# Adding the experts' rows in DRAM, spreading transposes and narrowing the stick-breaking attention in a two-model kernel

## The chip, the cores and the metric

The kernel runs on one core of a Trainium2 chip. The metric is the device time of one execution in microseconds (us). TensorE is called PE, VectorE DVE, ScalarE ACT, GpSimd POOL and SyncE SP; POOL and SP also issue DMAs, each from a queue of its own.

## The reference, cut to what matters

256 tokens of 1024 features go through a first block of two attention layers and then through a second block of two layers. In the second block the first layer has stick-breaking attention and a dense SwiGLU, the second has a blockwise attention and a mixture of eight experts, two per token. The change touches the stick-breaking attention and the mixture of experts:

```python
def stick_breaking_attention(q, k, v):            # per query block, all heads
    z = einsum('bhqd,bhkd->bhqk', qc, k) * scale
    past = k_pos[None, :] < q_pos[:, None]        # a query sees only earlier keys
    log_one_minus = where(past, log_sigmoid(-z), 0.0)
    after = cumsum(log_one_minus, reverse=True) - log_one_minus
    w = where(past, exp(log_sigmoid(z) + after), 0.0)
    return einsum('bhqk,bhkd->bhqd', w, v)

def moe_swiglu(t, w_router, w1, w3, w2):
    top_val, top_idx = top_k(t @ w_router, 2)
    gates = softmax(top_val) spread over the 8 experts
    y = sum over e of ((silu(t @ w1[e]) * (t @ w3[e])) @ w2[e]) * gates[:, e]
h = h + y;  out = rmsnorm(h, final_norm)
```

With 256 tokens and keys in two tiles of 128, the queries 0 to 127 see no key of the second tile: that quarter of the 256 x 256 table is always masked.

## The kernel before

All products are made in float32 precision from two rounded parts of each operand: a high part (a cast by ACT, tile names ending in `h` or index 0) and a remainder (`sub_lo` on DVE, `gsub_lo` on POOL, a subtraction of two SBUF operands), with three matmuls for each product (`mm3`). Every weight tile is loaded by SP, cast by ACT (line 85) and subtracted by DVE or POOL (line 86), and then used by PE. Every engine takes its instructions in program order, so the order of the code sets the order of the work on each queue.

The stick-breaking stage (lines 1447 to 1535) works through 16 heads, the units, in a software pipeline: `pipeline` runs the stages in a fixed order for each iteration i, each stage for the unit i minus its lag. A unit's table is [128 keys, 512]: columns 0 to 255 are the 256 queries for key tile 0, columns 256 to 511 the same queries for key tile 1. `scores` puts a mask into PSUM by a matmul (`identr`, `smask`, 512 columns) and adds the score products of two heads; `soft` makes the softplus by three ACT steps; `softplus` (DVE) adds and casts (`u`, `uh`); `softplus_lo` makes the remainder `ul` on POOL; `sums` adds the running sums by two matmuls of 512 columns (`ntri`) and two of 256 (`nones`); `weights` is an exponential on ACT; `split` makes `whh` and `wll` on DVE; `pv` multiplies by the values in six matmuls of 256 columns into the single PSUM buffer `o`; `out` copies `o` out by ACT and DVE (`og`). As `fill`, PE does the rest of the query and key projections (24 matmuls of 256 columns in each of the first iterations, which POOL ends with the remainders of `qT` and `kT`), then the first part of the output projection.

The dense layer that follows also writes zeros to a DRAM buffer `ysum` of 640 rows (lines 1578 to 1581, POOL). The mixture of experts begins with routing (lines 1793 to 2059): `posm` is each token's place in its expert's list, `G` a one-hot table of the first two experts, and 32 matmuls gather those experts' tokens (`pieces`). Beside that, `x_natural` turns the residual `xT` into rows of tokens by PE transposes, and ACT copies them into `hnat`.

Then 57 steps n run, one for each expert e and seventh f of its hidden width: `first(n)` (48 matmuls of 512 columns), `second(n-1)` (24 matmuls), and `turn(n)` (4 transposes of `hf`, line 1980). Each step uses six 1 MB weight tiles out of 13 staging tiles and, later, `xT` as a fourteenth (`Stream.staging`, `wm.ahead`). Small jobs wait in the list `later`; `first` takes one from it after each of its 8 chunks, `second` three after each of its 4. Jobs on that list: `rows_table` and `rows_of` (which find each slot's token row and its factor), `choices` (the gates by rank, `granks`), and `fetched`, whose four pieces transpose the rows that POOL fetched for the next two experts, with an ACT copy and a DVE subtraction each. The results of experts 0 to 5 are copied by ACT (`y`) and written by POOL's indirect DMA into `ysum`, a token's better expert into rows 0 to 255, its other one into rows 256 to 511 (line 2005). In the last two steps both halves are loaded back (line 2085), and four DVE instructions multiply them by `granks` and add them to `hnat` (line 2089). Experts 6 and 7 are added to `hnat` by PE and DVE directly (`scatter`).

Of the kernel before, what the change touches and what calls it, by code (L numbers as in the profile page):

```python
# [7 lines left out]
F = mybir.dt.float32  # L8
# [24 lines left out]
class Stream:  # L33
# [67 lines left out]
def tile_net(  # L101
# [1349 lines left out]
    stk = pa.tile([128, 768], R, name="stk", bufs=1)  # L1451
    vcopy(stk, stf)
    identr = pa.tile([128, 128], R, name="identr", bufs=1)
    vcopy(identr, ident)
    ntri, nones, smask = stk[:, 0:128], stk[:, 128:256], stk[:, 256:768]

    class UnitS:
        def __init__(self, j, h):
            self.j, self.h = j, h

        def scores(self):
# [3 lines left out]
            for u in us:  # L1465
                u.S = ps2p.tile([128, 512], F, tag="s2", name="s2")
                mm(u.S, identr, smask, True, False)
            for k in range(2):
                both_heads([u.S[:, k * T:(k + 1) * T] for u in us], [a[:, self.j, k * 128:(k + 1) * 128] for a in kT],
                           [a[:, self.j, :] for a in qT], False, k == 1)  # L1470

        def soft(self):
            self.u = u = pa.tile([128, 512], F, tag="u", name="u", bufs=3)
# [4 lines left out]
        def softplus(self):  # L1478
            u = self.u
            self.uh = pa.tile([128, 512], R, tag="uh", name="uh")  # L1480
            self.ul = pa.tile([128, 512], R, tag="ul", name="ul")
# [3 lines left out]
        def softplus_lo(self):  # L1485
            gsub_lo(self.ul, self.u, self.uh)

        def sums(self):
            o = self.S
            for n, a in enumerate((self.uh, self.ul)):  # L1490
                nc.tensor.matmul(o, ntri, a, start=False, stop=False, skip_group_check=True)
                nc.tensor.matmul(o[:, 0:T], nones, a[:, T:2 * T], start=False, stop=n == 1, skip_group_check=True)

        def weights(self):
            self.w = pa.tile([128, 512], F, tag="w", name="w", bufs=3)
            act(self.w, self.S, ACTF.Exp)

        def split(self):
            self.wh = pa.tile([128, 512], R, tag="whh", name="whh")
            self.wl = pa.tile([128, 512], R, tag="wll", name="wll")  # L1500
# [30 lines left out]
    for n in range(0, 16, 2):  # L1531
        units[n].other = units[n + 1]
    pipeline(units,
             (("fill", 0), ("pv", 6), ("sums", 3), ("weights", 4), ("scores", 0), ("soft", 1), ("softplus", 2), ("softplus_lo", 2), ("split", 5), ("out", 6)), fill)
# [28 lines left out]
    ysum = scr.tile([2 * T + 128, D], F, name="ysum")  # L1563
# [47 lines left out]
    pe = mp.enter_context(pool("moef0"))  # L1611
    wm.tiles = [None] * NS + [xT.rearrange("p k n -> p (k n)")]
# [136 lines left out]
    vals = pm.tile([128, 2, 8, 3], F, name="vals")  # L1749
    tcol = pm.tile([128, 4], F, name="tcol")  # L1750
    granks = pm.tile([128, 2, 2], F, name="granks")
# [90 lines left out]
    x_natural(0)  # L1842
# [15 lines left out]
    def rows_table():  # L1858
# [7 lines left out]
        ts(w, tcol[:, 0:1], 2.0 * T, ALU.add)  # L1866
        for t in range(2):
            ts(vals[:, t, :, 0], rank[:, t], 0.0, ALU.mult, tcol[:, t:t + 1], ALU.add)
            ts(vals[:, t, :, 2], rank[:, t], 0.0, ALU.mult, nrm[:, t:t + 1], ALU.add)
            stt(vals[:, t, :, 1], rank[:, t], 1.0 * T, posm[:, t], ALU.mult, ALU.subtract)  # L1870
            ts(vals[:, t, :, 1], vals[:, t, :, 1], tcol[:, t:t + 1], ALU.add, -2.0 * T, ALU.add)

    def choices():
        for c_ in range(2):
            stt(ex, rank, float(c_), gate, ALU.is_equal, ALU.mult)
            nc.vector.reduce_sum(out=granks[:, c_, :], in_=ex, axis=AX.X)
# [3 lines left out]
    def rows_of(e, g):  # L1880

        ps = bank("tp")
# [359 lines left out]
```

## Time and profile before

| | |
|---|---|
| Runs of the kernel before, median (3 runs) | 2032.65 us (2031.85 to 2034.75) |
| Profiled execution, its own time | 2035.86 us |
| Span of that execution in the trace | 2034.0 us |
| PE busy | 1943.6 us, 96% |
| DVE busy | 1592.9 us, 78% |
| ACT busy | 1310.9 us, 64% |
| POOL busy | 310.8 us, 15% |
| DMA traffic | 505.91 MB, 249 GB/s on the mean |

The rows count time from the first instruction of the span. The dense and expert layers fill most of it: the stick-breaking stage lies at about 606 to 697 us, routing at 1030 to 1050 us, the expert steps from 1050 us to the end. A row of the timeline gives the start, the duration, the engine, the line, the operation with its output and inputs, and in brackets how long the engine sat idle before it and for whose result. Matmuls overlap each other, so PE's pace is read from the distance between starts and not from a duration.

### The profile page before, as it was taken

To read this page: it belongs to the slowest core of one execution; us is meant where nothing else is said; L and a number is where in the kernel's file an instruction comes from. 1 tells how busy PE (TensorE), PEld (TensorE's weight loads), DVE (VectorE), ACT (ScalarE), POOL (GpSimd) and SP (SyncE) were. 2 spreads that over 40 slices of the span, in tenths; PEclk is the share of its full clock that TensorE was granted. 3 is DMA by queue.
4 is the path that set the end of the run, shared out by engine and by line. 5 is a ranking of instruction groups with operands and counts; after the bars stand their busy time and mean duration, and the time that the engine had idled before them with its cause. 6 is when DMAs were issued, how large, how long until landed. Compare 5 with 4: busy or idle time off the path is not lost. (4 is left out here: it accounts for less than half of the span.)

```text
span 2034.0 us, 29605 instructions
## 1 busy us (share of the span) xinstructions
PE 1943.6 (96%) x10970; PEld 1647.7 (81%) x10970; DVE 1592.9 (78%) x2096; ACT 1310.9 (64%) x1874; POOL 310.8 (15%) x390
## 2 busy tenths in 40 slices
PE   6999988999999899999989999999999999999996
PEld 3777777887878799998978888888888888888885
DVE  4576766348678867657769999999999999999997
ACT  3555544347657644445657787888778887788785
POOL 2123440005423321102520010000100001000000
PEclk8999998999999999999989999999999999999999
DMA  8343332445253265568669999999999999999990
GB/s 272 102 145 104 129 110 76 116 128 96 90 165 107 73 217 179 176 196 275 214 227 332 373 388 385 360 375 383 388 378 361 373 386 388 354 377 375 367 372 33
DMA packets 273463, 505.91 MB, mean 249 GB/s; under 512 B 23154, under 2 KB 108362, under 8 KB 273312
## 3 DMA queue, kind: packets, MB, share of 16 engines
q1 hardware_dynamic: 269856, 493.00, 69.1%
q0 software_dynamic: 3136, 10.41, 1.4%
q8 instruction: 88, 1.44, 0.3%
q14 instruction: 63, 0.52, 0.1%
q10 hardware_dynamic: 320, 0.53, 0.1%
HBM read 496.53 MB, written 7.37 MB: 248 GB/s over the span
## 5 line engine op out<-in xcount | busy, mean ns | idle before, releaser
L86 DVE TENSOR_TENSOR wl<-w,wh 128x1024 fp32r<-128x1024 f32 x624 | 753.3, 1228 | 59.0 <-ACT wh L85 19.6
L85 ACT CAST wh<-w 128x1024 fp32r<-128x1024 f32 x626 | 653.8, 1054 | 142.6 <-PE mm L130 102.3
L130 PE MATMUL mm<-wh,X 128*128 128x512 f32 x1792 | 570.6, 394 | 0.1
L130 PEld LDWEIGHTS mm<-wh,X 128*128 128x128 f32 x1792 | 337.2, 188 | 69.8 <-ACT hnat L138 0.3
L86 DVE TENSOR_TENSOR wl<-wf,wh 128x1024 fp32r<-128x1024 f32 x190 | 238.1, 1264 | 173.7 <-ACT wh L85 172.5
L130 PE MATMUL mm<-wl,X 128*128 128x512 f32 x896 | 349.4, 390 | 0.0
L85 ACT CAST wh<-wf 128x1024 fp32r<-128x1024 f32 x200 | 206.4, 1040 | 156.1 <-PE mm L130 131.5
L130 PE MATMUL y<-wh,hid 128*128 128x512 f32 x896 | 287.0, 390 | 1.5 <-DVE hid L144 0.8
L130 PEld LDWEIGHTS y<-wh,hid 128*128 128x128 f32 x896 | 168.1, 188 | 36.8 <-DVE hid L144 1.2
L130 PEld LDWEIGHTS mm<-wl,X 128*128 128x128 f32 x896 | 168.8, 188 | 33.4
L130 PE MATMUL y<-wl,hid 128*128 128x512 f32 x448 | 174.5, 389 | 2.1 <-DVE wl L86 2.1
L130 PE MATMUL mm<-hh,wh 128*128 128x256 f32 (+1 forms) x432 | 126.1, 292 | 5.1 <-ACT wh L85 3.2
L130 PE MATMUL mm<-hh,wl 128*128 128x256 f32 (+1 forms) x432 | 125.4, 290 | 1.3 <-DVE wl L86 1.2
L130 PE MATMUL mm<-hl,wh 128*128 128x256 f32 (+1 forms) x432 | 125.2, 290 | 0.0
L2005 POOL DMA_INDIRECT ysum<-y,rows x6 | 6.2, 1025 | 624.0 <-ACT y L138 479.2
L130 PEld LDWEIGHTS y<-wl,hid 128*128 128x128 f32 x448 | 84.1, 188 | 19.7 <-DVE wl L86 2.5
L130 PEld LDWEIGHTS mm<-hh,wh 128*128 128x128 f32 x432 | 83.2, 193 | 7.0 <-ACT wh L85 4.3
L154 POOL TENSOR_SCALAR e<-e,sm 128x512 f32<-128x512 f32 (+2 forms) x112 | 67.0, 609 | 125.2 <-DVE sm L847 115.0
L130 PEld LDWEIGHTS mm<-hh,wl 128*128 128x128 f32 x432 | 83.2, 193 | 2.5 <-DVE wl L86 1.9
L130 PEld LDWEIGHTS mm<-hl,wh 128*128 128x128 f32 x432 | 83.3, 193 | 0.6
L130 PE MATMUL fill<-hh,wh 128*128 128x256 f32 (+1 forms) x240 | 75.1, 313 | 1.2 <-DVE ev L144 0.7
L144 DVE TENSOR_TENSOR pt<-tp,pt 128x512 fp32r<-128x512 f32 (+2 forms) x80 | 41.5, 552 | 41.1 <-ACT pt L138 41.1
(377 smaller groups left out, 3488.8 us busy)
## 6 DMA issues: line engine op xcount, KB each, us to landing
w<-in_e_w_dram SPq DMA_DIRECT2D x313, 1024.0 KB, 7.5
wf<-in_w_dram SPq DMA_DIRECT2D x64, 512.0 KB, 4.7
wf<-in_w_mod_dram SPq DMA_DIRECT2D x48, 512.0 KB, 4.4
wf<-in_w_qkv_dram SPq DMA_DIRECT2D x48, 512.0 KB, 4.6
xT<-in_e_w_dram SPq DMA_DIRECT2D x23, 1024.0 KB, 7.2
wf<-in_b_w_in_dram SPq DMA_DIRECT2D x32, 512.0 KB, 3.8
wf<-in_a_w_in_dram SPq DMA_DIRECT2D x20, 512.0 KB, 4.1
wf<-in_w_o_dram SPq DMA_DIRECT2D x16, 512.0 KB, 3.4
```

Source lines behind the costliest of these rows:

```text
L85: nc.scalar.copy(out=hi[:, 0:m], in_=src)
L86: (low or nc.vector).tensor_tensor(out=lo[:, 0:m], in0=src, in1=hi[:, 0:m].bitcast(F), op=ALU.subtract)
L130: nc.tensor.matmul(o, l, r, start=start, stop=stop, **pos)
L144: (eng or nc.vector).tensor_tensor(out=o, in0=a, in1=b, op=op)
L154: nc.gpsimd.tensor_scalar(out=o, in0=i, scalar1=s, scalar2=1.0, op0=ALU.mult, op1=ALU.mult)
L2005: nc.gpsimd.indirect_dma_start(out=ysum, out_offset=rows(to, 1), in_=y, in_offset=None)
```

## The change

The stick-breaking table loses its always masked quarter: it becomes [128, 384], with 256 queries for key tile 0 and 128 for key tile 1. Mask, ACT and DVE steps are 384 wide; the `nones` matmuls, half of the score matmuls and half of the `pv` matmuls are 128 wide instead of 256. The remainder `ul` moves from POOL to DVE, right behind the cast. `o` becomes one tile with a half for each of two heads.

In the mixture of experts, `ysum` has 384 rows and is not zeroed. After the first step's `first` the residual is turned (`x_natural` for both halves), copied and written to `ysum` rows 0 to 255 by POOL's queue. An expert's result is multiplied by its gate in the ACT copy, and the indirect DMA adds it onto the rows in `ysum`; the rows of empty slots go to rows 256 to 383. At step (6, 2) one DMA on POOL's queue reads the 256 rows back into `hnat`. The loads at the end, `granks`, `choices` and the four DVE additions are gone. `xT` joins the staging tiles as the nineteenth load and not the fifteenth. `rows_table` waits for twelve chunks and not eight, and `rows_of` eight chunks more; for later experts it waits three chunks behind the one-hot table. The four transposing pieces of `fetched` are three places apart in `later`.

```diff
     def staging(self):
-            n = [0, total, *range(1, total)][(n - total) % (total + 1)]
+            k = self.spare
+            n = [*range(k), total, *range(k, total)][(n - total) % (total + 1)]
...
+    NQ = T + 128
+    o2 = pop.tile([128, 2, T], F, tag="o", name="o")
...
-                both_heads([u.S[:, k * T:(k + 1) * T] for u in us], [...],
-                           [a[:, self.j, :] for a in qT], False, k == 1)
+                both_heads([u.S[:, k * T:T + k * 128] for u in us], [...],
+                           [a[:, self.j, k * 128:T] for a in qT], False, k == 1)
...
-        def softplus_lo(self):
-            gsub_lo(self.ul, self.u, self.uh)
+            sub_lo(self.ul, u, self.uh)
...
-                nc.tensor.matmul(o[:, 0:T], nones, a[:, T:2 * T], ...)
+                nc.tensor.matmul(o[:, 128:T], nones, a[:, T:NQ], ...)
...
-            self.o = o = pop.tile([128, T], F, tag="o", name="o")
-            for k in range(2):
-                mm3(o, [v[:, k, j * 128:(j + 1) * 128] for v in vN],
-                    [w[:, k * T:(k + 1) * T] for w in (self.wh, self.wl)], k == 0, k == 1)
+            self.o = o = o2[:, self.h, :]
+            vh, vl = [[v[:, k, j * 128:(j + 1) * 128] for k in range(2)] for v in vN]
+            for k, (v, w) in ((k, a) for k in range(2) for a in ((vh, self.wh), (vh, self.wl), (vl, self.wh))):
+                nc.tensor.matmul(o[:, k * 128:T], v[k], w[:, k * T:T + k * 128], ...)
...
-    zero = tmp.tile([128, D], F, name="zero")
-    nc.gpsimd.memset(zero, 0.0)
-    for k in range(4):
-        nc.gpsimd.dma_start(out=ysum[k * 128:(k + 1) * 128, :], in_=zero)
...
+    wm.spare = 5
...
-    x_natural(0)
...
-            later.extend([lambda: None] * 8 + [rows_table, lambda: rows_of(0, g), choices])
+            later.extend([lambda: None] * 12 + [rows_table] + [lambda: None] * 8 + [lambda: rows_of(0, g)])
...
-                acopy(y[:, d * 512:d * 512 + 512], yps[d])
-            nc.gpsimd.indirect_dma_start(out=ysum, out_offset=rows(to, 1), in_=y, in_offset=None)
+                act(y[:, d * 512:d * 512 + 512], yps[d], ACTF.Copy, scale=at[to][1][:, 1, to % 2:to % 2 + 1])
+            nc.gpsimd.indirect_dma_start(out=ysum, out_offset=rows(to, 1), in_=y, in_offset=None, compute_op=ALU.add)
...
         if n == 1:
-            x_natural(1)
-            wm.ahead += 1
-            wm.load_to(wm.freed + wm.ahead)
             gates()
...
-        if n == 3:
-            for o, ps in xps[0:2]:
-                acopy(o, ps)
-    for o, ps in xps[2:]:
-        acopy(o, ps)
...
-                later.append(lambda g2=g2, e=e: rows_of(e + 1, g2))
+                later.extend([lambda: None] * 3 + [lambda g2=g2, e=e: rows_of(e + 1, g2)])
...
-                later.extend(pieces)
-            if n >= len(steps) - 2:
-                c_ = n - len(steps) + 2
-                sums[c_] = wm.staging().rearrange("p (t d) -> p t d", t=2)
-                nc.sync.dma_start(out=sums[c_], in_=ysum[c_ * T:(c_ + 1) * T, :].rearrange("(t p) d -> p t d", p=128))
-            if n == len(steps) - 1:
-                for c_ in range(2):
-                    for t in range(2):
-                        later.append(lambda c_=c_, t=t: stt(hnat[:, t, :], sums[c_][:, t, :], granks[:, c_, t:t + 1],
-                                                            hnat[:, t, :], ALU.mult, ALU.add))
+                for p_ in pieces:
+                    later.extend([p_, lambda: None, lambda: None])
+            if n == 0:
+                for t in range(2):
+                    x_natural(t)
+                    for o, ps in xps:
+                        acopy(o, ps)
+                    xps.clear()
+                    nc.gpsimd.dma_start(out=ysum[t * 128:(t + 1) * 128, :], in_=hnat[:, t, :])
+                assert wm.loaded == NS + wm.spare, wm.loaded
+                wm.ahead += 1
+                wm.load_to(wm.freed + wm.ahead)
+            if (e, f) == (NE - 2, 2):
+                nc.gpsimd.dma_start(out=hnat, in_=ysum[0:T, :].rearrange("(t p) d -> p t d", p=128))
```

## Rows read from the trace of the kernel before

**Rows 1.** Windows of the stick-breaking stage: span, then each engine's busy time, clock, DMA.

```profile
640.00:660.00 20.00, 18.92 (x151) 17.13 (x150) 19.16 (x26) 15.69 (x28) 8.78 (x8) 1.00 0.34 107
```

**Rows 2.** Timeline of DVE in the stick-breaking stage.

```profile
639.99 0.68 DVE L151 SCALAR_TENSOR_TENSOR u<-s,u 128x512 f32<-128x512 f32 x1
642.11 1.67 DVE L144 TENSOR_TENSOR wll<-w,whh 128x512 fp32r<-128x512 f32 x1
...
650.92 0.67 DVE L151 SCALAR_TENSOR_TENSOR u<-s,u 128x512 f32<-128x512 f32 x1
...
666.18 0.69 DVE L151 SCALAR_TENSOR_TENSOR u<-s,u 128x512 f32<-128x512 f32 x1
...
684.51 0.67 DVE L151 SCALAR_TENSOR_TENSOR u<-s,u 128x512 f32<-128x512 f32 x1
...
689.75 0.69 DVE L144 TENSOR_TENSOR wll<-w,whh 128x512 fp32r<-128x512 f32 x1
```

**Rows 3.** Timeline of POOL in the same stage.

```profile
640.17 1.62 POOL L144 TENSOR_TENSOR qT<-ev,qT 128x256 fp32r<-128x256 f32 x2 [2.87 <-ACT qT L138]
641.76 1.48 POOL L144 TENSOR_TENSOR ul<-u,uh 128x512 fp32r<-128x512 f32 x1
...
691.73 2.72 POOL L86 TENSOR_TENSOR wl<-wf,wh 128x1024 fp32r<-128x1024 f32 x1 [3.48 <-ACT wh L85]
```

**Rows 4.** Timeline of PE: running sums here, scores of the other attention at 943.

```profile
640.09 0.40 PE L1491 MATMUL s<-uh,stk 128*128 128x512 f32 x1
640.33 0.28 PE L1492 MATMUL s<-uh,stk 128*128 128x256 f32 x1
...
943.35 0.96 PE L130 MATMUL s<-kT,qT 64*128 64x128 f32 x12
...
943.73 0.57 PE L130 MATMUL s<-kT,qT 64*128 64x256 f32 x6
```

**Rows 5.** Waits from 606 to 695 us: total, times, longest.

```profile
PEld o L130 <- DVE og L144: 9.2, 7, 2.9
```

**Rows 6.** Timeline of PE in the first two expert steps.

```profile
1063.04 0.66 PE L1980 MATMUL tp<-cs,hf 128*128 128x128 f32 x4 [1.65 <-DVE hf L144]
...
1068.06 0.36 PE L130 MATMUL tp<-vals,G 128*128 128x3 f32 x2 [1.61 <-DVE vals L148]
...
1084.57 0.60 PE L1980 MATMUL tp<-cs,hf 128*128 128x128 f32 x4
```

**Rows 7.** A window in step 1, columns as in the first group.

```profile
1070.00:1071.00 1.00, 1.00 (x4) 0.71 (x3) 1.00 (x2) 0.00 (x0) 0.00 (x0) 0.50 0.84 317
```

**Rows 8.** Timeline of PE: the turns of two steps in a row, mid-stage.

```profile
1631.66 0.60 PE L1980 MATMUL tp<-cs,hf 128*128 128x128 f32 x4
...
1648.47 0.60 PE L1980 MATMUL tp<-cs,hf 128*128 128x128 f32 x4
```

**Rows 9.** Timeline of PE: the rows of experts 2 and 3.

```profile
1204.47 1.13 PE L130 MATMUL tp<-vals,G 128*128 128x3 f32 x8 [0.30 <-DVE G L148]
```

**Rows 10.** Timeline of PE: the third piece of fetched, experts 2 and 3.

```profile
1285.85 0.66 PE L1920 MATMUL tp<-cs,xn 128*128 128x128 f32 x4 [1.14 <-DVE X L144]
```

**Rows 11.** Timeline of DVE in the last step.

```profile
2004.69 2.47 DVE L151 SCALAR_TENSOR_TENSOR hnat<-xT,granks,hnat 128x1024 f32<-128x1024 f32 x2
```

**Rows 12.** Timeline of PE in the last step.

```profile
2009.55 0.50 PE L130 MATMUL y<-wl,hid 128*128 128x512 f32 x1 [2.06 <-DVE wl L86]
...
2013.62 0.73 PE L130 MATMUL y<-wh,hid 128*128 128x512 f32 x2 [0.80 <-DVE hid L144]
```

**Rows 13.** The page: rate in 40 slices; landing of the expert weights.

```profile
GB/s 272 102 145 104 129 110 76 116 128 96 90 165 107 73 217 179 176 196 275 214 227 332 373 388 385 360 375 383 388 378 361 373 386 388 354 377 375 367 372 33
...
w<-in_e_w_dram SPq DMA_DIRECT2D x313, 1024.0 KB, 7.5
```

**Rows 14.** Waits of SP's queue in the expert steps: total, times, longest.

```profile
SPq L58 <- DVE wl L86: 761.7, 316, 7.1
```

**Rows 15.** Instructions of line 2005, the indirect DMA into ysum.

```profile
DMA to landing us min/median/max: 5.5/6.9/7.8
```

More of the change, by code (lines that the diff above doesn't have):

```diff
@@ L1491, in sums @@
                 nc.tensor.matmul(o, ntri, a, start=False, stop=False, skip_group_check=True)
-                nc.tensor.matmul(o[:, 0:T], nones, a[:, T:2 * T], start=False, stop=n == 1, skip_group_check=True)
+                nc.tensor.matmul(o[:, 128:T], nones, a[:, T:NQ], start=False, stop=n == 1, skip_group_check=True)
         def weights(self):
-            self.w = pa.tile([128, 512], F, tag="w", name="w", bufs=3)
+            self.w = pa.tile([128, NQ], F, tag="w", name="w", bufs=3)
             act(self.w, self.S, ACTF.Exp)
         def split(self):
-            self.wh = pa.tile([128, 512], R, tag="whh", name="whh")
-            self.wl = pa.tile([128, 512], R, tag="wll", name="wll")
+            self.wh = pa.tile([128, NQ], R, tag="whh", name="whh")
+            self.wl = pa.tile([128, NQ], R, tag="wll", name="wll")
             vcopy(self.wh, self.w)
@@ L1505, in pv @@
             j = self.j
-            self.o = o = pop.tile([128, T], F, tag="o", name="o")
-            for k in range(2):
-                mm3(o, [v[:, k, j * 128:(j + 1) * 128] for v in vN],
-                    [w[:, k * T:(k + 1) * T] for w in (self.wh, self.wl)], k == 0, k == 1)
+            self.o = o = o2[:, self.h, :]
+            vh, vl = [[v[:, k, j * 128:(j + 1) * 128] for k in range(2)] for v in vN]
+            for k, (v, w) in ((k, a) for k in range(2) for a in ((vh, self.wh), (vh, self.wl), (vl, self.wh))):
+                nc.tensor.matmul(o[:, k * 128:T], v[k], w[:, k * T:T + k * 128], start=k == 0 and v is vh and w is self.wh,
+                                 stop=k == 1 and v is vl, skip_group_check=True)
         def out(self):
@@ L1533, in tile_net @@
     pipeline(units,
-             (("fill", 0), ("pv", 6), ("sums", 3), ("weights", 4), ("scores", 0), ("soft", 1), ("softplus", 2), ("softplus_lo", 2), ("split", 5), ("out", 6)), fill)
+             (("fill", 0), ("pv", 6), ("sums", 3), ("weights", 4), ("scores", 0), ("soft", 1), ("softplus", 2), ("split", 5), ("out", 6)), fill)
     begun.finish(1)
@@ L1562, in tile_net @@
     htok = scr.tile([T, D], F, name="htok")
-    ysum = scr.tile([2 * T + 128, D], F, name="ysum")
+    ysum = scr.tile([T + 128, D], F, name="ysum")
     rb33 = tmp.tile([33, 16], F, name="rb33")
@@ L1748, in tile_net @@
     cnt = pm.tile([128, 8], F, name="cnt")
-    vals = pm.tile([128, 2, 8, 3], F, name="vals")
+    vals = pm.tile([128, 2, 8, 4], F, name="vals")
     tcol = pm.tile([128, 4], F, name="tcol")
-    granks = pm.tile([128, 2, 2], F, name="granks")
     most_i = pm.tile([128, 1], mybir.dt.int32, name="most_i")
@@ L1865, in rows_table @@
         ts(tcol[:, 1:2], tcol[:, 0:1], 128.0, ALU.add)
-        ts(w, tcol[:, 0:1], 2.0 * T, ALU.add)
+        ts(w, tcol[:, 0:1], 1.0 * T, ALU.add)
         for t in range(2):
@@ L1869, in rows_table @@
             ts(vals[:, t, :, 2], rank[:, t], 0.0, ALU.mult, nrm[:, t:t + 1], ALU.add)
-            stt(vals[:, t, :, 1], rank[:, t], 1.0 * T, posm[:, t], ALU.mult, ALU.subtract)
-            ts(vals[:, t, :, 1], vals[:, t, :, 1], tcol[:, t:t + 1], ALU.add, -2.0 * T, ALU.add)
-    def choices():
-        for c_ in range(2):
-            stt(ex, rank, float(c_), gate, ALU.is_equal, ALU.mult)
-            nc.vector.reduce_sum(out=granks[:, c_, :], in_=ex, axis=AX.X)
+            stt(vals[:, t, :, 1], vals[:, t, :, 0], -1.0 * T, posm[:, t], ALU.add, ALU.subtract)
+        vcopy(vals[:, :, :, 3], gate)
     at = {}
@@ L1908, in fetch @@
         nc.gpsimd.indirect_dma_start(out=v, out_offset=None, in_=htok, in_offset=rows(e, 0))
-        gscale(v, v, at[e][1][:, e % 2:e % 2 + 1])
+        gscale(v, v, at[e][1][:, 0, e % 2:e % 2 + 1])
         return v
@@ L2059, in tile_net @@
     xn = {}
-    sums = {}
     nxt = ()
```

24 lines of the change are left out of this document (12 added, 12 removed).

## Prediction

> **What bounds the kernel now.** I read the page first, then windows over the stages that the change touches, then each engine's timeline in them, and the waits last. PE is the engine that is nearly always busy, and the expert steps are its own: two turns in a row are 16.81 us apart [rows 8], which is the pace of 72 matmuls of 512 columns and 4 transposes, with no wait between them. The weights are not the limit there: SP's queue waits 761.7 us in total for a staging tile to be freed by the subtraction on DVE [rows 14], so loads are ready ahead of their use. What the change can win lies therefore where PE waits. There are four such places: the stick-breaking stage, the first two expert steps, the steps with rows or transposes in between, and the last step.
>
> In the stick-breaking stage DVE is busy 19.16 of 20 us and PE 18.92 [rows 1]; a matmul row includes its fill and drain, so PE's share flatters it, and DVE sets the pace. One pair of units takes from 639.99 to 650.92, 10.93 us [rows 2].
>
> **Stick-breaking: DVE.** The subtraction `wll` takes 1.67 us beside POOL's `ul`, and 0.69 us at 689.75 [rows 2], in a stretch in which POOL sat idle for 3.48 us up to 691.73 [rows 3]. So most of `wll` is waiting for POOL. The change takes `ul` off POOL. Per unit I estimate three quarters of the width as three quarters of the time: `wll` 1.67 to 0.52 (-1.15), the add into `u` 0.68 to 0.55 (-0.13), and about 0.1 less for each of the two casts, an estimate in the same proportion; `ul` comes over at three quarters of 0.69, +0.52. That is -0.96 per unit, -1.9 per pair: DVE would need 9.0 us.
>
> **Stick-breaking: PE.** From start to start a matmul of 512 columns takes 0.24 us (640.09 to 640.33 [rows 4]), one of 256 half of that, 0.12. The price of a 128-column matmul over all 128 rows is not in the trace. Its nearest rows are six half-height ones of 128 columns in 943.35 to 943.73, 0.063 each [rows 4], two of which can share the array: so between 0.06 and 0.13 us; I take 0.07, since the row itself is nearer to that. The pair before: 48 fill matmuls 5.8, running sums 4 x 0.36 = 1.4, values 12 x 0.12 = 1.4, two masks 0.5, twelve scores about 0.9, 10.0 in all. After: sums 4 x (0.18 + 0.07) = 1.0, values 6 x (0.12 + 0.07) = 1.1, masks 0.36, scores 0.83, with fill 9.1 us; with 0.13 it is 9.7. PE's waits for the single `o` (weight loads alone 9.2 us in 7 waits [rows 5]) mostly end, since a head has its own half.
>
> So DVE at 9.0 and PE at 9.1 to 9.7 are level. POOL still makes the remainders of `qT` and `kT`, 1.62 us per pair [rows 3], beside DVE's subtractions. I take 9.5 us, a gain of 1.4 in each of the four full pairs (624 to 667 us): 5.7. The bounds are 9.1 (7.3) and 9.0 + 1.62 = 10.6 (1.3). The Trainium skill (SBUF — State Buffer, Who interferes with whom) says that an instruction of DVE with two SBUF inputs and one of POOL that reads SBUF exclude each other for the whole instruction. By that rule the moved `ul` meets all of the 1.62 us, and this part would give 1.3 and not 5.7.
>
> In the tail, without projections, five units of DVE take 666.18 to 684.51, 3.67 each [rows 2]. After: DVE 3.67 - 0.96 = 2.7, PE 12 x 0.12 for the output projection plus (9.1 - 5.8) / 2 = 3.1; I take 3.15, a gain of 0.5 x 5 = 2.6 (1.5 to 3.5). The first units are PE's already and the drain behind 684.5 holds waits for `og` of the kind in [rows 5]: together 2.0 (0.5 to 4). Sum of the stage: **10.3** (3.3 to 14.8).
>
> **The first two expert steps.** The first turn waited 1.65 us for DVE, and the next one comes at 1084.57, 21.53 us later [rows 6], 4.7 more than a plain step [rows 8]. In it PE waits 1.61 us for `vals` [rows 6], then runs at a granted clock of 0.50, the 1.2 GHz level [rows 7], after having stood still twice. The eight places more between `rows_table` and `rows_of` give DVE time for its small instructions, so the wait goes; the eight tiny matmuls stay (about 1.0, [rows 9]); the clock, I expect, stays up as PE no longer stands still there. 4.7 - 1.0 = 3.7. The 16 transposes of the residual go into the 1.65 us wait of the first turn; 0.36 per four (a turn), 1.4, so that they cost nothing there, and ACT's four copies fall into the time in which it waits for that turn. Before, they stood in the routing chain, PE's part of which waits mostly for DVE's one-hot; so little comes back, 0.7 (0 to 1). Together **4.4**; if the clock falls all the same, 1.5. POOL's two writes of the residual are behind nothing that PE waits for: POOL's next job is the fetch in step 9. The load of `xT`'s tile waits one step longer; twelve or more loaded tiles cover it.
>
> **Rows and transposes later.** `rows_of` waits 0.30 us for the one-hot in experts 2, 4 and 6 [rows 9]; three more places end that: **1.0** for the three (0.9 to 1.7 with the restart). The third piece of `fetched` waits 1.14 us for DVE's subtraction, as two banks serve four pieces [rows 10]; with one piece behind every six matmuls (1.4 us at the pace of [rows 8]) each finds a free bank. Three times that with some restart: **3.6** (3.0 to 4.3).
>
> **The last step.** DVE's four additions begin at 2004.69, and the first two take 2.47 us [rows 11]; weight remainders stand behind them, so PE waits 2.06 and then 0.80 us for the hidden tile's remainder [rows 12]. Without them both waits should all but end: **2.9** (2.1 to 3.6). The load back runs at step (6, 2), with 200 us to spare, and the zeroing ran on POOL with nobody waiting: both 0.
>
> **Accumulating DMA.** The trace has no add onto DRAM. The plain scatter lands in 5.5 to 7.8 us [rows 15]; nobody on the path waits for it, and the next user of `y` comes two steps later. It shares the 16 engines with the weights, so its price is what it takes from them. Below: 0, as the traffic of zeroing and of the two loads is gone too. Above: the rival below.
>
> Sum: 10.3 + 4.4 + 1.0 + 3.6 + 2.9 = 22.2 us (10.8 to 29.4). The profiled execution took 2035.86 us, 1.9 more than its span and 3.2 more than the median of the runs, 2032.65; it would take 2013.7. Against the median that is **2010.4 us**.
>
> **Rivals.** (A) POOL's remainders hold DVE as fully as `ul` did: the full pairs gain 1.3 and not 5.7, 2014.8 us. For it: `wll` beside POOL; against: POOL has one third of its work left there. 12%.
>
> (B) The clock falls elsewhere: PE now stands still from the routing matmuls to the one-hot with no transposes between, or in the wait of the first turn. 2.9 comes back, 2013.3 us. 9%.
>
> (C) The weights are at the ceiling of their rate already. Then the expert steps pay for each byte more: six adds read 0.5 MB each, and 3.1 MB at 388 GB/s [rows 13] are 8 us: 2018.4 us. Against it: the queue waits for tiles, not PE for loads [rows 14]. The Trainium skill (DMA: Bandwidth & Descriptors, Specifications) puts a core's share of HBM at about 358 GB/s, by which this case would hold; the slices of this trace at 373 to 388 GB/s [rows 13] speak against that figure. 4%.
>
> (D) Slower: an add holds the DMA engines for long, and the weight stream stands still behind it. A step uses six tiles, one per 2.80 us (16.81 / 6), and a tile takes 2.70 us at 388 GB/s, so 42 tiles between two adds win back 4.2 us; thirteen tiles less the 7.5 us of a landing [rows 13] are a lead of 29 us. With a pause d at each of six adds PE loses 6 x (d - 4.2) - 29 us. That eats the 22.2 us from d = 12.7 on, about twice the landing of the plain scatter [rows 15]; with d = 20 it is 66 us, 2076 us. Read and write of 0.5 MB each make about 1.5 to 3 us of traffic, so d would have to come from something other than bytes. 5%.
>
> **How the numbers follow.** The forecast as it stands has 67%; A, B and C are also faster, and 3% are left for changes that cancel out. A measurement of this kernel can tell 0.2%, 4 us, from no change. Faster: 67 + 12 + 9 + 4 = 92%; same 3%; slower 5%. The range takes in the bounds of the sum (2003.3 to 2021.9) and one us for the runs' spread: 2002 to 2022; it leaves out D and gains that I do not see.
>
> **What would show it.** Right: `wll` and `ul` at 0.5 to 0.6 us with no POOL beside them; stick-breaking about 10 us shorter; steps of 16.8 us throughout, with about 1 us more where `rows_of` and 2 us more where transposes stand; the first two turns 18 us apart with a clock of 1.00; no wait for `wl` in the last step. Wrong: matmuls of 128 columns no closer than those of 256; subtractions still above 1 us; PE or ACT waiting for weight loads behind an add.

## The result and the profile after

| | before | after |
|---|---|---|
| Runs, median (range) | 2033.24 us of 4 (2031.85 to 2034.75) | 2012.63 us of 4 (2008.50 to 2012.88) |
| Profiled execution, own time | 2035.86 us | 2008.50 us |
| Its span | 2034.0 us | 2006.6 us |
| PE busy | 1943.6 us | 1932.3 us |
| DVE busy | 1592.9 us | 1574.7 us |
| POOL busy | 310.8 us | 290.2 us |

The ratio of after to before is 0.9894, with a 95% interval of 0.9877 to 0.9911: 20.6 us less by the medians. The forecast was 2010.4 us (2002 to 2022).

The two profiles lie 27.4 us apart, more than the medians do. Part of that has nothing to do with the change: in the first 80 us, where both kernels have the same code, the granted clock differs from one execution to the next, and the start of all that follows with it. The cast that opens the stick-breaking stage starts at 605.82 us in the trace of before and at 602.20 in that of after, 3.6 us earlier; over the fourteen traces of this study it starts between 602.20 and 607.75, and nearly all of the difference is there by 80 us. The same window of three traces shows it, the third being the last experiment below, which has the code of after in this place (columns as in [rows 1]; before, after, last experiment):

```profile
20.00:40.00 20.00, 13.54 (x61) 5.59 (x60) 13.02 (x32) 7.23 (x15) 4.66 (x2) 0.79 0.78 263
```

```profile
20.00:40.00 20.00, 14.44 (x74) 6.30 (x72) 13.57 (x34) 6.93 (x13) 4.67 (x2) 1.00 0.87 289
```

```profile
20.00:40.00 20.00, 13.67 (x59) 5.59 (x60) 12.74 (x31) 6.93 (x13) 4.66 (x2) 0.80 0.75 260
```

So I compare places, from a marker at one end to a marker at the other. Where the clock stays up, these repeat within 0.1 us from trace to trace.

| place | before, us | after, us | gain | forecast |
|---|---|---|---|---|
| stick-breaking stage, first cast to first `xT` behind it | 97.02 | 86.26 | 10.8 | 10.3 |
| of it, eight units of the full pairs | 40.89 | 36.45 | 4.4 | 5.7 |
| of it, the last five units (tail) | 18.33 | 14.44 | 3.9 | 2.6 |
| of it, first units, lead and drain | 37.80 | 35.37 | 2.4 | 2.0 |
| from there to the first turn | 360.20 | 359.74 | 0.5 | 0.7 |
| first turn to second | 21.53 | 17.81 | 3.7 | 3.7 |
| three steps with `rows_of` | 55.55 | 53.72 | 1.8 | 1.0 |
| three steps with `fetched` | 59.92 | 55.89 | 4.0 | 3.6 |
| last step and the part behind it | 42.33 | 39.38 | 2.9 | 2.9 |
| sum of the places | | | 23.7 | 22.2 |

All other steps take 16.8 us in both, but for one that takes 18.78 before and 18.70 after. A window of 20 us in the stick-breaking stage of after, to be read beside [rows 1], a window of the first expert step in the place of [rows 7], where the clock is now 1.00, and the rate in the 40 slices of the page, as [rows 13]:

```profile
640.00:660.00 20.00, 17.95 (x152) 16.98 (x151) 18.64 (x36) 13.88 (x30) 3.09 (x4) 1.00 0.31 105
1050.00:1056.00 6.00, 6.00 (x29) 4.94 (x28) 5.56 (x6) 4.89 (x6) 0.00 (x0) 1.00 0.99 351
```

```profile
GB/s 287 102 137 106 130 112 70 124 127 100 84 157 125 84 182 181 178 196 280 213 218 396 366 384 394 367 388 368 385 392 360 389 370 395 370 376 394 374 359 23
```

Timeline of PE in one full pair of after: the running sums at both ends, the values and the scores between.

```profile
633.45 0.39 PE L1497 MATMUL s<-uh,stk 128*128 128x384 f32 x1
...
636.99 0.39 PE L1515 MATMUL o<-whh,vN 128*128 128x256 f32 x1
...
637.45 0.22 PE L1515 MATMUL o<-whh,vN 128*128 128x128 f32 x1
637.51 0.28 PE L1515 MATMUL o<-wll,vN 128*128 128x128 f32 x1
637.63 0.27 PE L1515 MATMUL o<-whh,vN 128*128 128x128 f32 x1
637.74 0.39 PE L1497 MATMUL s<-uh,stk 128*128 128x384 f32 x1
637.96 0.22 PE L1498 MATMUL s<-uh,stk 128*128 128x128 f32 x1
638.02 0.39 PE L1497 MATMUL s<-ul,stk 128*128 128x384 f32 x1
...
638.81 0.90 PE L131 MATMUL s<-qT,kT 64*128 64x256 f32 x12
...
643.24 0.39 PE L1497 MATMUL s<-uh,stk 128*128 128x384 f32 x1
```

From 633.45 to 643.24 are 9.79 us, and no row between has a bracket: PE never waits. In before a pair had one wait of about 0.5 us for `og`. DVE in the same pair:

```profile
633.42 0.55 DVE L152 SCALAR_TENSOR_TENSOR u<-s,u 128x384 f32<-128x384 f32 x1
634.00 0.60 DVE L142 CAST uh<-u 128x384 fp32r<-128x384 f32 x1
634.64 0.97 DVE L145 TENSOR_TENSOR ul<-u,uh 128x384 fp32r<-128x384 f32 x1
...
637.33 1.22 DVE L87 TENSOR_TENSOR wl<-wf,wh 128x1024 fp32r<-128x1024 f32 x1 [0.39 <-ACT wh L86]
...
639.71 0.56 DVE L145 TENSOR_TENSOR ul<-u,uh 128x384 fp32r<-128x384 f32 x1
640.57 0.56 DVE L145 TENSOR_TENSOR wll<-w,whh 128x384 fp32r<-128x384 f32 x1
643.21 0.55 DVE L152 SCALAR_TENSOR_TENSOR u<-s,u 128x384 f32<-128x384 f32 x1
```

`wll` now takes 0.56 us instead of 1.67 [rows 2]. The first cast and `ul` lie beside POOL's remainder of `qT` and are 0.24 and 0.41 us longer than in the second unit (0.36 and 0.56). DVE idles 0.39 us in the pair: PE is full and DVE nearly so.

PE in the expert steps of after: the first two turns, the rows of experts 2 and 3, a piece of `fetched`, and the last step, to be read beside [rows 6, 9, 10, 12].

```profile
1048.20 0.66 PE L1978 MATMUL tp<-cs,hf 128*128 128x128 f32 x4
1062.34 0.95 PE L131 MATMUL tp<-vals,G 128*128 128x4 f32 x8
1066.01 0.60 PE L1978 MATMUL tp<-cs,hf 128*128 128x128 f32 x4
...
1189.49 0.95 PE L131 MATMUL tp<-vals,G 128*128 128x4 f32 x8
...
1268.11 0.60 PE L1918 MATMUL tp<-cs,xn 128*128 128x128 f32 x4
...
1984.04 0.60 PE L1978 MATMUL tp<-cs,hf 128*128 128x128 f32 x4
1985.31 0.50 PE L131 MATMUL y<-wh,hid 128*128 128x512 f32 x1 [0.67 <-ACT hid L139]
```

The waits of 1.65, 1.61, 0.30, 1.14 and 2.06 us are gone; one of 0.67 is left. Between 1060 and 2007 us PE waits for nothing but `hid`, `hnat` and `y`, 1.4 us in all.

### The profile page after: what moved, and what is told of

Same layout as the page of the kernel before. It is cut to its first block, busy times and chain, and to the rows that moved or that the text cites. A ratio compares the mean times of both kernels' runs of the same rounds, so it can differ in the third digit from the quotient of the medians.

```text
span 2006.6 us, 29582 instructions
## 1 busy us (share of the span) xinstructions
PE 1932.3 (96%) x10970; PEld 1643.1 (82%) x10970; DVE 1574.7 (78%) x2104; ACT 1305.2 (65%) x1874; POOL 290.2 (14%) x372
## 3 DMA queue, kind: packets, MB, share of 16 engines
HBM read 495.48 MB, written 6.32 MB: 250 GB/s over the span
```

## The experiments

The three questions: do the parts add up; what in the stick-breaking stage brought the gain, DVE's relief or PE's shorter work; and does the accumulating DMA cost anything. "Stage" is the first row of the table above. Gains by the median are against the kernel before as measured in the same hour.

**One part of the change at a time.** First the stick-breaking part alone, on the kernel before.

> The kernel before with the stick-breaking part of the change alone (narrow table, ul on DVE, a half of o for each head). Theory: the parts add up. The stage, from the cast of stk to the first xT behind it, takes 97.02 us in the trace of before and 86.26 in that of after; here it takes 86.3 (85.5 to 87), everything behind it stays as before (21.5 us in the first expert step, 19.1 in the last), and the time is 10 to 11 us under the kernel before. Rival: the stage sets PE and the loads behind it differently, and part of the gain is given back ahead of the experts; then the stage is as short, and the time is less than 8 us under the kernel before.

Measured: 2025.05 us, ratio 0.9959 (0.9946 to 0.9971), 8.3 us under before (5.9 to 11). The stage took 86.27 us; the three steps with rows 18.33 to 18.86 and the last step 19.13, as in before. The gain lies under the 10 to 11 that I gave, close to the 8 of the rival, and the interval holds both. The trace differs from that of before in two places behind the stage. The way to the first turn took 361.72 us and not 360.20. In its routing the clock is at the lower level for longer (0.53 in 1019 to 1037 us, in before 0.53 in 1035 to 1046), which may be why; no run separates it. And the first expert step took 19.93 us and not 21.53, with the same wait for `vals`, 1.60 us. A window of that step, this run first and then the run with bunched places below, where the clock fell:

```profile
1056.00:1058.00 2.00, 1.15 (x9) 1.10 (x10) 1.93 (x9) 0.17 (x1) 0.00 (x0) 1.00 0.77 203
```

```profile
1056.00:1058.00 2.00, 2.00 (x7) 1.62 (x7) 1.52 (x5) 0.00 (x0) 0.00 (x0) 0.61 1.05 422
```

The move without narrowing, further below, has the code of before in this step and took 21.55 us. So behind a wait of 1.6 to 1.8 us the clock falls in some executions and not in others, of the same code too, and where it falls the step is 1.6 us longer.

Then the changes to the experts alone:

> The changed kernel with the stick-breaking part of the kernel before. Theory: the parts add up; the stage takes 97 us, the first expert step 17.8, the steps with rows 17.75, those with transposes 18.6, and the last part is 2.95 shorter; these places add up to 13.0 us between the two traces, and the medians leave 9.8 (20.6 less 10.8): 9.5 to 13 us under the kernel before. Rival: something that these places do not show (traffic of the adds, the later load of the fourteenth tile) costs time elsewhere; then less than 9.

Measured: 2022.65 us, ratio 0.9945 (0.9928 to 0.9962), 11.2 us under before. The stage took 96.98 us, the first expert step 17.81, the steps with rows 17.74 to 18.23, those with transposes 18.62 to 18.65. 8.3 and 11.2 make 19.5 us, beside 20.6 for the whole change: the parts add up, within their intervals.

**Narrowing without the move.**

```diff
             vcopy(self.uh, u)
-            sub_lo(self.ul, u, self.uh)
+        def softplus_lo(self):
+            gsub_lo(self.ul, self.u, self.uh)
```

> The changed kernel with the remainder ul back on POOL, in the narrow width: narrowing without the move. Theory (POOL and DVE keep each other out): wll, 0.56 us in the trace of after, goes to about 1.25 (three quarters of 1.67), ul leaves DVE (0.56 to 0.97 less), and DVE's unit comes out about as long as or 0.2 us longer: the stage takes 86 to 90 us. Rival: with less work in each the two run side by side; wll stays under 0.8, DVE is free for 0.56 us per unit, and the stage stays at 86.3 or falls below, since PE then sets the pace at 9.1 to 9.7 us per pair.

Measured: 2012.09 us, ratio 0.9897 (0.9880 to 0.9913), no different from the changed kernel; the stage 87.32 us, 1.06 more. DVE, the end of one unit:

```profile
642.59 0.35 DVE L142 CAST whh<-w 128x384 fp32r<-128x384 f32 x1
642.97 1.26 DVE L145 TENSOR_TENSOR wll<-w,whh 128x384 fp32r<-128x384 f32 x1
```

`wll` is back at 1.26 us, three quarters of 1.67: it waits for POOL's `ul` as before. But the unit is hardly longer, since DVE now makes no `ul`. What POOL held up (1.26 - 0.56 = 0.70 us) and what DVE would have to do itself (0.56) are nearly the same.

**The move without narrowing.** In the kernel before, `gsub_lo` of `ul` becomes `sub_lo`.

> The kernel before with ul on DVE instead of POOL, at the full 512 columns: the move without the narrowing. Theory: wll falls from 1.67 to 0.69 us, ul costs 0.69 on DVE, so DVE's unit is 0.3 us shorter and a pair takes 10.0 to 10.4 us instead of 10.93, where PE's own 10.0 us stop it: the stage takes 92 to 95 us instead of 97. Rival: POOL's remainders of qT and kT meet the moved subtraction for their full 1.62 us per pair; then the move alone gives nothing, 96 to 99 us.

Measured: 2031.39 us, ratio 0.9983 (0.9974 to 0.9993), 3.5 us under before; the stage 94.34 us, 2.7 less than before. `wll` takes 0.69 us and `ul` 0.69, or 1.11 beside POOL; a pair takes 10.72 us, not the 10.0 to 10.4 that I gave. Of the 10.8 us of the stage the move alone brings 2.7, or 1.06 once the table is narrow; narrowing alone (with the second half of `o`) brings 9.7, or 8.1 once `ul` has moved.

**Which engine sets the pace now?** First 0.45 us more for PE per pair:

```diff
                 mm(u.S, identr, smask, True, False)
+                mm(u.S, identr, smask, False, False)
```

> The changed kernel with 0.45 us more work for PE per pair of units: the mask matmul of each unit stands twice (0.22 us from start to start, at the pace of the running sums of 384 columns). Theory A (PE sets the pace of the full pairs, whose matmuls follow each other without a gap in the trace of after): the four full pairs take 10.2 to 10.3 us instead of 9.79; the tail, where DVE has no idle time, stays at 2.91 us per unit. Theory B (DVE sets the pace, as the prediction had it): the pair stays at 9.8.

Measured: 2014.71 us in a single execution. A full pair takes 10.15 us (637.25 to 647.40 on DVE), 0.36 more; the tail stays at 2.80 to 3.06 us per unit but for one unit of 4.34 at half clock. The four masks:

```profile
642.14 0.93 PE L131 MATMUL s<-stk,identr 128*128 128x384 f32 x4
643.00 0.39 PE L131 MATMUL s<-qT,kT 64*128 64x256 f32 x2
```

From the first mask to the scores are 0.86 us, 0.36 more than the 0.50 of the changed kernel (638.31 to 638.81) and not the 0.45 that I had reckoned. So PE's addition came through in full, and PE has no wait in this pair either. Then 0.72 us more for DVE per pair:

```diff
-            vcopy(self.uh, u)
+            for _ in range(2):
+                vcopy(self.uh, u)
```

> The changed kernel with 0.36 us more work for DVE per unit: the cast uh is made twice. Theory A (PE sets the pace of the full pairs): the pair stays within 0.2 us of 9.79, since DVE idles 0.39 us ahead of a weight remainder and has little else to spare; the tail units, DVE's, go from 2.91 to 3.27 us. Theory B (DVE sets the pace): the pair takes 10.5 us.

Measured: 2017.99 us in a single execution; the pair takes 10.22 us, 0.43 more. POOL's remainder now falls on the casts and no longer on `ul`:

```profile
642.17 0.76 DVE L142 CAST uh<-u 128x384 fp32r<-128x384 f32 x2
643.03 0.56 DVE L145 TENSOR_TENSOR ul<-u,uh 128x384 fp32r<-128x384 f32 x1
...
647.08 1.45 DVE L142 CAST uh<-u 128x384 fp32r<-128x384 f32 x2
```

In the unit without POOL the casts take 0.40 us more than in the changed kernel, in the one beside it 0.83 more, and there `ul` takes 0.41 less: 0.82 us more for DVE per pair. Its idle time of 0.39 us is gone, which leaves the 0.43 that the pair lost; PE now waits 0.32 us for `og`. So neither theory holds alone: PE sets the pace of the changed pairs, and DVE is only 0.39 us behind it. The sum of the prediction had them level too, at 9.0 and 9.1 to 9.7.

**A single buffer `o`.**

```diff
-            self.o = o = o2[:, self.h, :]
+            self.o = o = pop.tile([128, T], F, tag="o", name="o")
```

> The changed kernel with the single buffer o of before. Theory: a value matmul waits again for og of the unit before it, as in before, where PE idled 0.48 us for it and lost about 0.6 in each full pair: pairs of 10.2 to 10.4 us, the stage 2 to 4 us longer than 86.3. Rival: DVE, relieved by the narrow table, has og ready in time, and the stage stays at 86.3; then the second half of o is worth nothing.

Measured: 2012.99 us in a single execution. The full pairs stay at 9.79 us: with the narrow table `og` is ready in time, and my theory fell. The stage is 88.51 us all the same, 2.25 more, in one place. PE waits there 2.05 us for `og`, and then:

```profile
659.41 0.58 PE L1514 MATMUL o<-whh,vN 128*128 128x256 f32 x1 [2.05 <-DVE og L145]
```

```profile
659.00:661.00 2.00, 1.59 (x7) 1.60 (x8) 1.76 (x5) 1.68 (x5) 0.00 (x0) 0.51 0.00 0
661.00:663.00 2.00, 2.00 (x8) 1.56 (x9) 1.86 (x6) 0.84 (x2) 0.00 (x0) 0.50 0.03 8
```

The clock is at its lower level, 1.2 GHz, until 665.9 us, and DVE, which sets the pace there, stands still for PE's result:

```profile
666.97 0.43 DVE L145 TENSOR_TENSOR og<-o,og 64x256 fp32r<-64x256 f32 x1 [2.27 <-ACT og L139]
```

The changed kernel waits as long in this place, 2.04 us, and goes on at 1.00:

```profile
656.59 0.38 PE L1515 MATMUL o<-whh,vN 128*128 128x256 f32 x1 [2.04 <-DVE og L145]
```

```profile
656.00:658.00 2.00, 1.42 (x11) 1.42 (x12) 1.73 (x5) 1.94 (x5) 0.00 (x0) 1.00 0.01 5
```

The same edit a second time:

> The kernel with the single buffer o once more, to tell a loss of the buffer from one of the clock. In its first run the full pairs stayed at 9.79 us, and the whole loss of 2.25 us lay at 659.4 to 665.9 us, where the granted clock was 0.50 behind PE's wait of 2.05 us for og; the changed kernel has the same wait (2.04 us) and 1.00 behind it. Theory A (the clock falls by chance of the execution): this profile may show 86.3 or 88.5 us for the stage, and the median lies within 1.5 us of the changed kernel's 2012.6. Theory B (the single buffer brings the fall, by what it does to PE's work ahead of the wait): the stage takes 88.5 us again with 0.50 in the same place, and the median is 2 us or more above 2012.6.

Measured: 2013.27 us (2011.55 to 2013.99), ratio 0.9888 (0.9871 to 0.9904), 0.6 us from the changed kernel's median. Its stage took 88.60 us, with 0.50 in the same place. So the traces speak for theory B (fallen in both with the single buffer, in none of the seven traces that have both halves of `o` and no extra work in this stage), and the median for A. Behind the stage 0.5 us come back: from there to the first turn the two traces have 359.18 and 359.25 us, the changed kernel 359.74. By the places 1.7 to 1.9 us are left, and the interval (19.5 to 26.3 us under before) holds that as well as nothing. Whether the second half of `o` is worth 2 us or nothing stays open.

**The accumulating DMA.** First without it: `compute_op=ALU.add` is taken off the indirect write.

> The changed kernel with the plain indirect write in place of the accumulating one; the sum of the two experts and the residual is thereby left out of rows whose expert is 0 to 5. Theory (the add is hidden): landing falls from 8.7 us to about 7, steps at 16.8 and the last part stay as they are, and the median stays within 2 us of the changed kernel's 2012.6. Rival (the add costs bandwidth or holds the weight stream): six adds fewer save 2 us or more, seen in the steps behind an add.

Measured: 2011.08 us (2010.15 to 2013.94), ratio 0.9893 (0.9877 to 0.9910), beside 0.9894 with the add. From the first turn to the last the steps take 935.81 us, with the add 935.84. The add lands later (median 8.7 us, with the plain write 7.2) and occupies POOL for 1.60 us instead of 1.05; PE waits for neither.

Then with more of them: behind each of the six adds stand four more onto a second buffer.

> The changed kernel with four further accumulating writes of the same rows, onto a second DRAM buffer, behind each of the six adds: 24 adds more. Theory (an add costs the weight stream its bytes, and the lead of the stream takes that in): by the sum of the prediction PE loses 6 x (d - 4.2) - 29 us for a pause d per expert; four adds with 0.5 MB written each are 2 MB, 5.4 us at 388 GB/s, so nothing is lost (0 to 2 us); if each also reads 0.5 MB of DRAM, 10.8 us and 11 us lost, 2023 us. Rival (an add holds the DMA engines for its landing of 8.7 us): 35 us per expert and 156 us lost, 2169 us. What tells them apart are PE's waits for weight loads in the expert steps, of which after has none.

Measured: 2029.56 us, 16.9 above the changed kernel's 2012.63 (15.5 by the ratios, 0.9970 and 0.9894); the steps take 954.75 us together, 18.9 more than in the changed kernel. The steps behind the first three experts' adds lose nothing. Step 31 loses 2.7 us, steps 37 to 39 lose 7.9, steps 44 and 45 lose 8.2 (beside the 1 MB that is read back into `hnat`, and with the clock at 0.91 in 1820 to 1840 us). That looks like a lead which is used up and then a full price per expert. ACT and PE now wait for weights (waits of 1690 to 1840 us):

```profile
ACT wh L86 <- DMA w<-in_e_w_dram: 24.1, 21, 5.3
PEld mm L131 <- ACT wh L86: 5.5, 4, 3.5
```

With a steady loss of 8.0 us per expert and the 4.2 that the stream wins back, five adds hold it for 12.2 us, 2.4 each: an estimate, which rests on two experts. With it the formula of the prediction gives 6 x (12.2 - 4.2) - 29 = 19 us; 18.9 were measured, which bears out the lead of 29 us. The packets of POOL's queue say about the same (packets, MB, share of 16 engines' span; the changed kernel, then this run):

```profile
q0 software_dynamic: 3120, 10.41, 1.8%
q0 software_dynamic: 6864, 24.05, 5.0%
```

That is 65 us more for 24 adds and 1 MB of first rows, about 2.6 per add. 2.4 to 2.6 us are the time of 0.95 to 1.0 MB at 388 GB/s, so an add seems to cost its bytes, 0.5 MB written and as much read. The profile counts only what is written (HBM read 495.48 MB in both), so the reading is argued and not shown. My expectation of 11 us left the original add out of the pause; with it, and with 1.05 MB for each add, the formula gives 27, which is too much.

**Places in the list of small jobs, as before.**

```diff
-                for p_ in pieces:
-                    later.extend([p_, lambda: None, lambda: None])
+                later.extend(pieces)
...
-            later.extend([lambda: None] * 12 + [rows_table] + [lambda: None] * 8 + [lambda: rows_of(0, g)])
+            later.extend([lambda: None] * 8 + [rows_table, lambda: rows_of(0, g)])
...
-                later.extend([lambda: None] * 3 + [lambda g2=g2, e=e: rows_of(e + 1, g2)])
+                later.append(lambda g2=g2, e=e: rows_of(e + 1, g2))
```

> The changed kernel with the places in the list of small jobs as before: rows_table after eight chunks with rows_of right behind it, rows_of of later experts right behind the one-hot, the four transposing pieces without places between them. Theory: the waits come back where they were; steps with rows 18.35 us instead of 17.74, those with transposes 19.97 instead of 18.63, so 5.8 us in the six steps; the first expert step takes 19.9 us with the clock staying up, as in the run with the stick-breaking part alone, or 21.5 with the clock falling, as in the trace of before. Sum 8 to 9.5 us over the changed kernel. Rival: the gated ACT copy and the four-column vals changed the waits too, and the six steps lose less than 4 us.

Measured: 2020.81 us, 8.2 above the changed kernel's 2012.63 (7.7 by the two ratios to before, 0.9932 and 0.9894). The steps with rows took 18.35, 18.37 and 18.82 us, those with transposes 19.98, 19.96 and 19.98, the first step 21.42 with the clock fallen (window above). The waits are back in their places:

```profile
1054.96 1.06 PE L131 MATMUL tp<-vals,G 128*128 128x4 f32 x8 [1.79 <-DVE vals L142]
...
1272.44 0.66 PE L1918 MATMUL tp<-cs,xn 128*128 128x128 f32 x4 [1.14 <-DVE X L145]
```

**The residual's work, as before.** `x_natural` and its copies go back into the routing, and the two loads and four additions into the last two steps:

```diff
+            if n >= len(steps) - 2:
+                c_ = n - len(steps) + 2
+                sums[c_] = wm.staging().rearrange("p (t d) -> p t d", t=2)
+                nc.sync.dma_start(out=sums[c_], in_=ysum[0:T, :].rearrange("(t p) d -> p t d", p=128))
+            if n == len(steps) - 1:
...
+                        later.append(lambda c_=c_, t=t: stt(hnat[:, t, :], sums[c_][:, t, :], tcol[:, 3:4],
+                                                            hnat[:, t, :], ALU.mult, ALU.add))
```

> The changed kernel with two things of before: the 16 transposes of the residual and ACT's four copies stand in the routing again, and the last two steps load two halves and DVE makes four additions of 128x1024 (here with the factor 0 on the summed rows, so that the output stays the same). Theory: the last step takes 19.1 us instead of 16.8 and the part behind the last turn 23.2 instead of 22.55: 2.9 us; ahead of the first turn 0.5 to 0.8 us come back; the first expert step stays at 17.8. In all 3.4 to 3.7 us. Rival: the last part stays at 16.8, because it was the multiplication by granks or its place, not the four additions, that held the weight remainders; then under 1.5 us.

Measured: 2016.51 us (2014.39 to 2018.25), 3.9 above the changed kernel's 2012.63 (3.1 by the ratios, 0.9909 and 0.9894). The last step took 19.16 us, the way to the first turn 0.4 more, the first step 17.81. The part behind the last turn took 25.2 us and not 23.2: behind the waits of 2.06 and 0.68 us the clock fell in this execution, which it did not in that of before.

```profile
1986.06 0.50 PE L131 MATMUL y<-wl,hid 128*128 128x512 f32 x1 [2.06 <-DVE wl L87]
1988.92 0.79 PE L131 MATMUL y<-wh,hid 128*128 128x512 f32 x1 [0.68 <-ACT hid L139]
```

```profile
1987.00:1989.00 2.00, 1.32 (x8) 0.79 (x6) 2.00 (x3) 0.72 (x2) 0.00 (x0) 0.61 0.00 0
1989.00:1991.00 2.00, 2.00 (x4) 1.20 (x5) 2.00 (x3) 1.76 (x2) 0.00 (x0) 0.50 0.00 0
```

## Why the prediction was right, and where its steps were not

The forecast of 2010.4 us is 2.2 from the median, well within its range, and what it named as signs of being right came: `wll` and `ul` at 0.56 us away from POOL, the first two turns 17.8 us apart, a clock of 1.00 behind them, no wait for `wl` in the last step. By its steps:

**Stick-breaking, 10.3 forecast, 10.8 measured, by a different division; that the sum fits so well is partly luck.** The full pairs gave 4.4 us and not 5.7: a pair takes 9.79 us and not 9.5. PE's part was priced too low: values 1.1 (measured 0.75 and 0.64 for two units, 1.4), masks 0.36 (0.50), sums 1.0 (two times 0.57), fill 5.8 (5.9). The 0.07 us that I took for a matmul of 128 columns holds only for one behind a wider one (637.45 to 637.51 behind 256 columns, 637.96 to 638.02 behind 384, 0.06 each). The next two of the three value matmuls, each with other weights, take 0.11 to 0.12 (637.51, 637.63, 637.74), no less than those of 256. The three together take 0.29 us, 0.10 each, between the two bounds; the sign of being wrong, matmuls of 128 columns no closer than those of 256, came half true. The prediction says that the trace of before has no such matmul over all 128 rows, but it has: the four transposes of a turn are of 128 columns and take 0.60 us together [rows 8]. One alone lasts 0.27 (as at 637.63), so they start 0.11 apart, and the eight of four columns at 1189.49 above, 0.95 us together, are not much closer.

The tail gave 3.9 and not 2.6: it is DVE's there (no idle time between its rows, 2.80 and 3.02 us in turn, where I had 2.7), and not PE's as I had it at 3.15.

PE's waits for `o` went from 8.5 to 4.7 us in the stage. I put that down to the second half of `o`, but the pairs lose their wait with the single `o` too: it is the narrow table that has `og` ready in time.

In before, and in the two other traces with the wide table, PE waits 2.5 to 2.7 us for `og` at the head of the tail, and the clock falls behind it, which I hadn't seen in the trace; windows of before:

```profile
666.00:668.00 2.00, 1.79 (x9) 1.70 (x10) 1.80 (x5) 1.81 (x4) 0.42 (x1) 0.66 0.04 8
668.00:670.00 2.00, 2.00 (x9) 1.25 (x10) 2.00 (x3) 0.60 (x1) 0.90 (x1) 0.50 0.02 4
```

That is 2 x 0.34 + 2 x 0.50 = 1.7 us of full clock lost to PE, but hardly any of it to the stage. DVE sets the pace of this tail, and in its five units it idles once:

```profile
673.21 0.43 DVE L144 TENSOR_TENSOR og<-o,og 64x256 fp32r<-64x256 f32 x1 [0.22 <-ACT og L138]
```

So about 0.2 us of the stage's gain are the clock's. With the narrow table, where DVE needs 2.9 us per unit and not 3.67, a fall as long cost a unit 1.3 us (4.34 and not 3.06, in the run with the mask twice).

**DVE and POOL.** I put `ul`'s move first among the reasons and it is the smallest: narrowing alone brings 9.7 of the 10.8 us. The reading that `wll` waits for POOL was right (1.67, 1.26 and 0.56 us in three kernels), and the 0.52 us that `ul` costs DVE stood in the sum. What the sum didn't divide is the 1.15 us off `wll`: 0.41 of them come with the narrow table alone, and with `ul` at 0.56 the move is worth 1.26 - 0.56 - 0.56 = 0.14 us per unit. Rival A expected POOL's remaining 1.62 us per pair to come on DVE in full. They cost 0.65 (0.24 on the cast and 0.41 on `ul`). The rule of the Trainium skill (SBUF — State Buffer, Who interferes with whom) names the right pair of engines (it counts casts among those that can contend, and the cast here does). The 10.6 us that the prediction worked out by it took the whole of POOL's time as DVE's loss; the loss came out smaller, 0.65 us for the two POOL instructions of 1.54 us together, as if each of DVE's had waited only for what was left of POOL's. That last reading is argued and not shown.

**First two expert steps, 4.4 forecast, 4.2 measured.** The waits are gone, and the clock stays up. About 1.6 us of it come from the clock, and the executions of the old code above show that this part is not there every time. Rival B is out: the clock is at its lower level in the routing of both (0.53 in 1035 to 1046 us before, 0.54 in 1020 to 1035 after), but the way to the first turn is no longer for it, and from 1035 us on the clock is 1.00.

**`rows_of`, 1.0 forecast, 1.8 measured.** The term was mis-sized. I took the idle time in the bracket, 0.30 us [rows 9]; only the upper bound of 1.7 allowed for a restart. From the matmul ahead of `rows_of` to the one behind it are 1.69 us in before (1203.77 to 1205.46) and 1.03 in after (1189.27 to 1190.30), 0.66 less. Of the 0.36 that the bracket doesn't count, about half lies ahead of the idle time (the last wide matmul's row runs for 0.40 us, where the next one otherwise starts after 0.23) and half behind it (from the first of the eight to the next wide matmul 0.99 us and not 0.81). The run with the places undone gives the same 0.6 per step.

**Transposes 3.6, measured 4.0; last step 2.9, measured 2.9.** Both by the mechanism forecast; the runs that undo them bring the waits back at the same instruction and length.

**The accumulating DMA, 0 forecast, 0 measured.** Rival C is out: the weights are not at a ceiling (slices up to 396 GB/s, and six adds change no step). Rival D's form was right and the price that it needed far off: a pause of about 2.4 us per add and not 12.7, so that one add per expert is less than the 4.2 us won back, and five are not.

**What stays open.** The places sum to 23.7 us and the medians lie 20.6 apart, with an interval of 18 to 25 us that holds both. The profiled execution of before lost 1.6 us to a fall of the clock in the first expert step, which is missing in another execution of the same code; that would explain a part of the difference, but executions without a profile don't show where their time went.

## What to carry to other kernels

When a helper engine's work blocks the main one, compare what the block costs with what the main engine would pay to do that work: here the two were nearly equal, and it was less work (the masked quarter) that paid. Price a wait by the distance between the full-rate instructions on both sides of it, not by the idle time alone, and look at the granted clock behind PE's long waits (1.6 to 2.7 us here), in more than one execution; what a fall costs depends on which engine sets the pace there. A background transfer was free here as long as the stream it delays won its time back before the next one; its pause against that time is what to work out.

## What the runs showed of the hardware that was not expected

- A matmul of 128 columns behind one of 256 or 384 is followed after 0.06 us. Behind another of 128, with other weights each, it is followed only after 0.11 to 0.12, like those of 256 columns.
- I had counted on the subtractions alone, but a cast on DVE is held up by POOL's subtraction too. In the tail of after, `uh` takes 1.76 us instead of 0.36 while POOL makes a remainder of 128x1024:

```profile
671.64 1.76 DVE L142 CAST uh<-u 128x384 fp32r<-128x384 f32 x1
```

```profile
670.78 2.40 POOL L87 TENSOR_TENSOR wl<-wf,wh 128x1024 fp32r<-128x1024 f32 x1 [15.99 <-ACT wh L86]
```

- The same PE wait of about 2 us is followed by a granted clock of 1.00 in some kernels and executions and of 0.50 in others. Where PE set the pace or DVE was close to it, a fall cost 1.3 to 2.3 us here; in the tail of before, where DVE had 3.67 us of work per unit, 0.2.
- An indirect write that adds lands 1.5 us later than a plain one (8.7 and 7.2 us) and occupies POOL's issue for 1.60 us instead of 1.05.
